# The first FFN product of a hybrid decoder layer, ordered by one event loop

## The chip, the core and the metric

The kernel runs on one core of a Trainium2 chip. The time is device time in microseconds (us) of that core, from launch to end; a median of several runs is compared. Five engines work side by side, each through its own queue in order: TensorE (PE) multiplies matrices, with PEld as its weight load; VectorE (DVE), ScalarE (ACT) and GpSimd (POOL) work elementwise; SyncE (SP) issues most of the memory transfers (DMAs), ACT some of them. SBUF is the on-chip memory of the operands; PSUM holds the products in banks.

## What is computed

One layer on 2048 tokens of width 1024: a norm and a combined projection, three mixers side by side (sliding-window attention, a state-space scan, sparse attention), an output projection, and a feed-forward network (FFN). The part that matters here is the FFN, in float32:

```python
h2 = rms_norm(x, norm2_g[l])
hid = jax.nn.relu(jnp.einsum('bld,df->blf', h2, w_up[l]))        # 2048 x 1024 by 1024 x 4096
x = x + jnp.einsum('blf,fd->bld', hid * hid, w_down[l])          # 2048 x 4096 by 4096 x 1024
```

## The kernel before, in words

**Seven products for eight.** Both FFN products cut their operands in two by two blocks and form seven block products, called "1" to "7" and made in the order `ORDER = "1675243"`. For each, one token operand (a "factor") and one weight operand are needed. Factors "1", "2", "3" are blocks of the normed rows, turned (in memory: `hT`); "4" to "7" are sums of blocks (in memory: `sums`). Weight operands "1", "2", "4" are blocks of `w_up`; the other four are sums that GpSimd forms.

**Three matmuls for one.** A float32 operand is split into a high half in the matmul's rounded format (a cast on ACT) and a low half (source minus high, on DVE). Each 128 by 512 piece of a product is high times high, high times low and low times high. A block product has four such pieces, so twelve matmuls.

**Steps.** The first product (`phase_up`, line 1999) works on 1024 tokens at a time (p = 0, then 1) and 256 columns of `w_up` at a time (f): 32 steps of seven products. For p = 0, f runs downwards, for p = 1 upwards, so that steps 15 and 16 share their weights. The seven factors of a token half stay in SBUF (`fh`, `fl`); the weights of each step are loaded (`ur`, line 2117), summed (`fs`, line 2121) and split (`uh`, `ul`, lines 2128 and 2131). Products go to four banks a, d, c, b in two sets that alternate by step; "1" and "2" share bank a, "7" and "4" bank c, "5" and "3" bank b. The evictions take one bank after another: ACT copies "1" (line 2186), DVE adds the others (`add`, line 2175) into result buffers, ACT or DVE applies relu and square (lines 2178, 2179, 2201, 2202), and GpSimd combines the four results into the factors "5", "6", "7", "3" of the second product (`ev`, line 2182), which go to memory (`vd`, line 2172). The four blocks of results take eight result buffers a step out of ten; three more hold running sums (`eu`).

**The first factors.** A factor is loaded whole, 1 MB, into one of two buffers (`fx`, line 2078). Those of the first three products are split in four pieces of 512 (lines 2086 and 2090, from lines 2084 to 2090 `high` and `low`); the other four of p = 0 are split whole, 2048 wide, by `refill`. At the change of half, `refill` splits the factors of p = 1 as each product of step 15 has released its factor; three of them come in four pieces of 256 KB (`fy`, line 2106) in free weight buffers.

**Rows of the second half.** During the first twelve steps, `fetch` (line 2042) loads normed rows (`fxr`), ACT scales them (line 2050), TensorE turns them (line 2059), ACT scales them again (`fxb`, line 2061), GpSimd forms their sums (`fxt`, line 2071), and SP stores both.

**What sets the order.** The attention and the output projection before the FFN (`phase_mix`, line 1156) are written as tasks of an event loop (`Flow`, line 1067): each task yields operations with an engine and an expected time, and the loop issues whichever operation can start first by these times, the lowest rank first among equals. What it issues stays in that order on each engine (`manual_schedule`). In the kernel before, the loop also takes in the FFN's first pieces: `attention_over` (line 1863), `ffn_factor` (1888), `ffn_weights` (1903), `ffn_kept` (1912) and `ffn_product` (1918), up to step 0's products "1", "6" and "7". The rest of `phase_up` is written as plain loops, and the framework's scheduler chooses the order on each engine. `phase_down` (line 2272), the second product, is left to the scheduler too; its first loads and splits are raised in priority by 1000 instructions (`DOWN_HOIST`), so that they may go between the last instructions of the first product. Its buffers lie on bytes of the first product's.

## Time and profile before

| | us |
|---|---|
| median of 3 runs (2465.37 to 2467.47) | 2465.64 |
| the profiled execution's own time | 2468.63 |
| its span, first to last instruction | 2466.8 |
| TensorE busy in it | 2399.6 |
| first product, 32 steps: from 1196 to 1845 | 649 |
| second product: from 1845 to the end | 622 |

A row of the profile names the engine, the line of the code, the operation and the tiles (written <- read), and how long it took; in square brackets stands how long its engine had been idle before and what it had waited for. `<-DVE fl L2090` means that the last thing to arrive was a tile `fl` written by VectorE at line 2090. Rows of a stretch give each engine's busy time with the number of its instructions that lie in or reach into it, the clock that TensorE was granted (1.00 is full), and the share of DMA time.

### The profile page before, as it was taken

How to read it: one execution, taken by the hardware profiler on the slowest of the kernel's cores; microseconds unless marked ns; L12 is line 12 of the kernel's file. 1: busy time of each engine (PE TensorE's matmuls, PEld its weight loads, DVE VectorE, ACT ScalarE, POOL GpSimd, SP SyncE). 2: the span in 40 equal slices, each digit the busy share in tenths (PEclk: the TensorE clock that was granted, in tenths of full speed). 3: DMA queues.
4: the chain of work that ended last, by engine and by line, in shares of the span. 5: the costliest groups of instructions: out<-in, count | busy, mean ns of one | idle time of the engine just before them, and what ended most of it. 6: DMA issues, size and time to landing. Idle time of an engine off the chain costs nothing.

```text
span 2466.8 us, 37987 instructions
## 1 busy us (share of the span) xinstructions
PE 2399.6 (97%) x12738; PEld 2061.1 (84%) x12738; DVE 1776.0 (72%) x3473; ACT 1322.2 (54%) x2765; POOL 1038.4 (42%) x1070
## 2 busy tenths in 40 slices
PE   8999998999999999999999999999999999999999
PEld 8899998777788888989787788788887888888887
DVE  7853875864687888888656566655558888889886
ACT  6443545765677767666465556444444444434442
POOL 0000223322343454321656674666554544445447
PEclk9999999999899999999999999999999999999999
DMA  7483334441332243211676667655548443444435
GB/s 238 135 259 116 107 93 109 107 152 50 96 97 70 87 129 114 63 44 53 206 221 190 189 197 219 195 154 153 156 129 284 128 124 107 126 135 130 127 102 197
DMA packets 402260, 344.45 MB, mean 140 GB/s; under 512 B 43622, under 2 KB 359020, under 8 KB 400112
## 3 DMA queue, kind: packets, MB, share of 16 engines
q1 hardware_dynamic: 341696, 288.23, 38.8%
q10 hardware_dynamic: 60368, 53.80, 7.0%
q8 instruction: 100, 1.64, 0.3%
q14 instruction: 96, 0.79, 0.1%
HBM read 227.39 MB, written 119.76 MB: 141 GB/s over the span
## 4 chain that ended last, share of the span: by engine, by line
PE 71%; DVE 2%; issue 2%; DMA 2%; POOL 1%; ACT 1%; SPq 0%; ACTq 0%; DVEq 0%; POOLq 0%
PE pdc L2360 7%; PE pdb L2360 7%; PE pda L2360 7%; PE pw L1802 7%; PE pub L2151 6%; PE puc L2151 6%; PE pua L2151 6%; PE pdd L2360 3%; PE pud L2151 3%; PE pos L1497 3%; PE pps L1464 2%; PE pqs L1439 1%; PE pqs L1440 1%; PE pow L1497 1%; PE ppw L1464 1%
## 5 line engine op out<-in xcount | busy, mean ns | idle before, releaser
L1995 ACT CAST v<-vr 128x512 fp32r<-128x512 f32 x224 | 139.2, 623 | 303.9 <-DMA vr<-vd 149.8
L1996 DVE TENSOR_TENSOR v<-vr,v 128x512 fp32r<-128x512 f32 x224 | 240.4, 1082 | 75.3 <-ACT v L1995 75.1
L2360 PE MATMUL pdc<-dw,v 128*128 128x512 f32 x768 | 187.5, 393 | 4.1 <-ACT dw L1995 3.2
L2360 PE MATMUL pdb<-dw,v 128*128 128x512 f32 x768 | 184.5, 389 | 0.0
L2360 PE MATMUL pda<-dw,v 128*128 128x512 f32 x768 | 184.5, 389 | 0.0
L2360 PEld LDWEIGHTS pdc<-dw,v 128*128 128x128 f32 x768 | 145.5, 190 | 35.8 <-ACT dw L1995 3.7
L548 POOL TENSOR_TENSOR t<-Q,E 128x508 f32<-128x508 f32 x16 | 21.3, 1334 | 365.6 <-ACT Q L528 334.7
L2360 PEld LDWEIGHTS pdb<-dw,v 128*128 128x128 f32 x768 | 144.3, 188 | 30.0
L2360 PEld LDWEIGHTS pda<-dw,v 128*128 128x128 f32 x768 | 144.1, 188 | 29.9
L2121 POOL TENSOR_TENSOR fs<-ur,ur 128x512 f32<-128x512 f32 x62 | 92.9, 1499 | 161.1 <-DMA ur<-in_w_up 135.2
L2128 ACT CAST uh<-fs 128x512 fp32r<-128x512 f32 x124 | 76.3, 621 | 152.7 <-PE pub L2151 57.3
L2131 DVE TENSOR_TENSOR ul<-fs,uh 128x512 fp32r<-128x512 f32 x124 | 128.3, 1035 | 38.5 <-ACT uh L2128 38.1
L2131 DVE TENSOR_TENSOR ul<-ur,uh 128x512 fp32r<-128x512 f32 x93 | 96.6, 1040 | 40.4 <-ACT uh L2128 38.6
L1480 ACT CAST ths<-pps 128x512 fp32r<-128x512 f32 (+1 forms) x144 | 78.7, 562 | 67.2 <-PE pps L1464 62.2
L2182 POOL TENSOR_TENSOR ev<-e,e 128x512 f32<-128x512 f32 x64 | 94.5, 1476 | 42.8 <-ACT e L2179 18.5
L1485 DVE TENSOR_TENSOR tls<-pps,ths 128x512 fp32r<-128x512 f32 (+1 forms) x144 | 93.1, 657 | 23.1 <-ACT ths L1480 22.1
L1802 PE MATMUL pw<-wo_h,mh 128*128 128x512 f32 x256 | 106.5, 416 | 1.0 <-DVE mx L1824 0.5
L2151 PE MATMUL pub<-fh,uh 128*128 128x512 f32 x256 | 102.1, 399 | 4.6 <-DVE e L2175 3.0
L1802 PE MATMUL pw<-wo_l,mh 128*128 128x512 f32 x256 | 104.4, 408 | 0.0
L1802 PE MATMUL pw<-wo_h,ml 128*128 128x512 f32 x256 | 103.7, 405 | 0.0
L2151 PE MATMUL pub<-fl,uh 128*128 128x512 f32 x256 | 101.1, 395 | 0.3 <-DVE fl L2090 0.3
L2151 PE MATMUL pub<-fh,ul 128*128 128x512 f32 x256 | 101.0, 394 | 0.0
(583 smaller groups left out, 7778.4 us busy)
## 6 DMA issues: line engine op xcount, KB each, us to landing
vr<-vd SPq DMA_DIRECT2D x224, 256.0 KB
vd<-ev SPq DMA_DIRECT2D x128, 256.0 KB
ur<-in_w_up SPq DMA_DIRECT2D x124, 256.0 KB
vd<-e ACTq DMA_DIRECT2D x64, 256.0 KB
dr<-in_w_down SPq DMA_DIRECT2D x32, 512.0 KB
x<-in_x SPq DMA_DIRECT2D x16, 512.0 KB
mx<-in_x ACTq DMA_DIRECT2D x32, 256.0 KB
x<-mx ACTq DMA_DIRECT2D x32, 256.0 KB
```

The costliest lines, as they stand in the source:

```text
L1480: yield "ACT", cast_ns(n), lambda: nc.scalar.copy(th[:, 0:nb], pt[:, 0:nb])
L1485: t = yield "DVE", sub_ns(n), lambda: nc.vector.tensor_tensor(tl[:, 0:nb], pt[:, 0:nb], th[:, 0:nb], op=ALU.subtract)
L1497: nc.tensor.matmul(po_of(), v_of(b0 + j), tt[:, j].rearrange("p h q -> p (h q)"), start=b0 + j == 0 and n == 0, stop=b0 + j == nblk - 1 an ...
L1802: t = yield "PE", mm_ns(512), lambda: nc.tensor.matmul(pw[n], a[half][:, j], b[k][:, sl], start=k == 0 and m == 0, stop=k == NK - 1 and m ...
L1995: nc.scalar.copy(dh, src)
L1996: nc.vector.tensor_tensor(dl, src, dh, op=ALU.subtract)
L2121: nc.gpsimd.tensor_tensor(S[n], x, y, op=op)
L2128: nc.scalar.copy(res[o][0], source(o))
L2131: nc.vector.tensor_tensor(res[o][1], source(o), res[o][0], op=ALU.subtract)
L2151: nc.tensor.matmul(bank, w[:, k], h[o][:, k], start=first and k == 0 and n == 0, stop=k == HALF - 1 and n == 2, skip_group_check=True)
L2182: nc.gpsimd.tensor_tensor(tile_("v" + o), x, y, op=op)
L2360: nc.tensor.matmul(bank[b, q], x[:, q, j], y[:, j], start=first and j == 0 and n == 0, stop=j == 1 and n == 2, skip_group_check=True)
```

## The change

The generator `phase_up` becomes a class `Up` whose parts are all tasks of the same event loop; the whole first product is now issued in the loop's order.

- **Order of products.** Steps 0 and 1, and steps 16 and 17, are interleaved: three products of the first step, then by turns one of the second and one of the first, then the last three of the second.
- **Factors.** Every factor of both halves is split in four pieces of 512; a product may begin when its first piece is there. In p = 0, all seven are fetched by a task of their own (`first_factors`), each as soon as one of the two buffers is free. In p = 1 (`second_factors`), the fetches begin from step 13 on, when the rows are stored: "1" and "6" whole into the two buffers, "7" and "5" in pieces in weight and sum buffers, "2", "4" and "3" whole as the buffers come free.
- **Weights.** `all_weights` loads those of step n + 1 when step n begins, into the same six buffers; each of the fourteen split halves has a buffer of its own name.
- **Results.** One pool of 13 buffers; seven are used in a step (the running sum is kept in the buffer of result "12", and "7" overwrites it).
- **Rows of the second half.** `sums` loads after the last product of step 3m; scaling and turning are tied to products that are done and to the expected landing. For m = 0 the turning moves to steps 2 and 3.
- **Room.** The output projection's buffers (`late_pool`) are released inside the loop (`late_over`) once every block's rows are stored; the later factors, the result buffers and the second set of banks are laid out then (`rest`). Until then only products "1" and "6" of step 0 may be issued; all evictions wait for it in the loop.

```diff
@@ -1864,62 +1868,26 @@
 
             yield E[NT - 1]["oc"]
             yield R["pt"]
...
             t = yield "SP", 30, switch
             put(R["pt"], t)
             put(R["pw"], t)
...
+            up.begin(flow, E[NT - 1]["mh", 0], t)
+            for i in range(NT):
+                yield E[i]["x1"]
+                if i < NT // 2:
+                    yield E[i]["hT"]
+            yield sums_out
+            t = yield "SP", 30, late_over
+            up.rest(t)
+
+        def late_over():
+            c_late.close()
...
+class Up:
...
+        self.steps = [(0, f) for f in reversed(range(nf))] + [(1, f) for f in range(nf)]
+        self.turned_at = nf
+        self.order = []
+        for n in range(2 * nf):
+            if n in (0, nf):
+                self.order += [(n, 0), (n, 1), (n, 2)] + [x for k in range(4) for x in ((n + 1, k), (n, k + 3))] + [(n + 1, k) for k in (4, 5, 6)]
+            elif n not in (1, nf + 1):
+                self.order += [(n, k) for k in range(7)]
+        self.due = {x: 10 * j for j, x in enumerate(self.order)}
...
+    def begin(self, flow, hold, t):
+        self.flow, self.hold = flow, hold
+        self.hp, self.hh, self.hl = {}, {}, {}
...
+        self.factors(ORDER[:1])
+        self.s = Slots(flow, self.pool("f_st", 5), "s", 5)
+        self.x = Slots(flow, self.pool("f_x", 2), "x", 2)
+        self.ur = Slots(flow, self.pool("f_ru", 6), "ur", 6)
...
+        sp(self.all_weights(), R_FFN, t)
+        sp(self.first_factors(), R_FFN, t)
+        sp(self.products(), 2 * R_FFN, t)
+        sp(self.second_factors(), self.rank(self.turned_at - 1, 0), t)
+        for m in range(4):
+            sp(self.sums(m), self.rank(max(3 * m + 1, 2), 0) + 50, t)
+
+    def rest(self, t):
+        flow = self.flow
+        self.v = Slots(flow, self.pool("f_e", 13), "e", 13)
+        self.g2t = self.pool("f_g", 1).tile([P, PAD], F32, name="f_g2")
+        self.factors(ORDER[3:])
+        self.ps.append(self.pool("f_psu2", 1, space=PSUM))
+        self.nc.sync.dma_start(self.g2t[:, 0:NK], self.g2[0].rearrange("(k p) -> p k", p=P))
+        flow.fire(self.more, t)
...
+    def all_weights(self):
+        flow, made = self.flow, Event()
+        for n in range(len(self.steps)):
+            if n == self.turned_at:
+                continue
+            if n > 1:
+                yield self.began[n - (2 if n in (2, self.turned_at + 1, self.turned_at + 2) else 1)]
+            if n == self.turned_at + 1:
+                yield self.pieces
+            f0 = self.steps[n][1] * FC_UP
+            A = {}
+            for q, uses in (("11", 3), ("21", 2), ("22", 2), ("12", 2)):
+                k, c = int(q[1]) - 1, f0 + P * (int(q[0]) - 1)
+                A[q] = yield from self.ur.get([P, HALF, P], f"ur{n}{q}", uses)
+                t = yield "SP", 60, lambda: self.nc.sync.dma_start(
+                    A[q].tile, self.w_up[0, 512 * k:512 * k + 512, c:c + P].rearrange("(k p) f -> p k f", p=P))
+                A[q].land = self.landing(t, 2.6e5)
+            if n == self.turned_at - 1:
+                flow.fire(self.last_loads, t)
+            flow.spawn(self.weight_sums(n, A), self.rank(n, 1) - 5, t)
+            for o, q in (("1", "11"), ("2", "12"), ("4", "22")):
+                flow.spawn(self.keep(n, o, A[q], A[q].land), self.rank(n, ORDER.index(o)), 0.0)
+
...
+    def weight_sums(self, n, A):
+        S = {}
+        for e in A.values():
+            yield e.land
+        if n == 0:
...
+                                     (3, "11", "21", ALU.subtract, 1, "7"), (4, "12", 2, ALU.subtract, 1, "3")):
+            S[j] = yield from self.s.get([P, HALF, P], f"fs{n}{j}", uses)
+            a, b = S.get(x) or A[x], S.get(y) or A[y]
+            t = yield "POOL", 1400, lambda: self.nc.gpsimd.tensor_tensor(S[j].tile, a.tile, b.tile, op=op)
+            a.drop(t)
+            b.drop(t)
+            e = Event()
+            self.flow.fire(e, t)
+            self.flow.spawn(self.keep(n, o, S[j], e), self.rank(n, ORDER.index(o)), t)
+
...
+    def keep(self, n, o, src, there):
+        yield there
+        yield self.room[o]
+        h, l = self.W[n][o] = [self.up_.tile([P, HALF, P], F32R, tag=q + o, name=f"{q}{n}{o}", bufs=1) for q in ("uh", "ul")]
+        yield "ACT", 621, lambda: self.nc.scalar.copy(h, src.tile)
+        t = yield "DVE", 900, lambda: self.nc.vector.tensor_tensor(l, src.tile, h, op=ALU.subtract)
+        src.drop(t)
+        self.flow.fire(self.made[n][o], t)
+
...
+    def halves(self, p, o, rank, parts):
+        if p:
+            yield self.done[self.turned_at - 1][ORDER.index(o)]
+        elif o in ORDER[3:]:
+            yield self.more
+        h, l = self.hh[p, o], self.hl[p, o] = [self.hp[o].tile([P, HALF, 4, P], F32R, tag=n + o, name=f"f{n}{p}{o}") for n in "hl"]
+        for k in range(HALF):
+            src, x, land = parts[k]
+            yield land
+            t = yield "ACT", 621, lambda: self.nc.scalar.copy(h[:, k], x)
+            self.flow.spawn(self.low_half(p, o, k, src, x, h, l), rank, t)
+
+    def low_half(self, p, o, k, src, x, h, l):
+        t = yield "DVE", 950, lambda: self.nc.vector.tensor_tensor(l[:, k], x, h[:, k], op=ALU.subtract)
+        src.drop(t)
+        self.flow.fire(self.fact[p, o][k], t)
+
+    def whole(self, p, o, rank):
+        src = yield from self.x.get([P, HALF, 4, P], f"fx{p}{o}", HALF)
+        t = yield "SP", 60, lambda: self.nc.sync.dma_start(src.tile, self.source(p, o))
+        land = self.landing(t, 1e6)
+        self.flow.spawn(self.halves(p, o, rank, [(src, src.tile[:, k], land) for k in range(HALF)]), rank, t)
+
+    def in_pieces(self, p, o, slots, rank):
+        parts = []
+        for k in range(HALF):
+            src = yield from slots.get([P, 4, P], f"fy{p}{o}{k}", 1)
+            t = yield "SP", 60, lambda: self.nc.sync.dma_start(src.tile, self.source(p, o)[:, k])
+            parts.append((src, src.tile, self.landing(t, 2.6e5)))
+        self.flow.spawn(self.halves(p, o, rank, parts), rank, t)
...
+    def first_factors(self):
+        for k, o in enumerate(ORDER):
+            yield from self.whole(0, o, self.rank(0, k))
+
+    def second_factors(self):
+        n = self.turned_at - 1
+        yield self.began[n - 2]
+        for e in self.turned:
+            yield e
+        rank = [self.rank(n + 1, k) for k in range(7)]
+        yield from self.whole(1, ORDER[0], rank[0])
+        yield from self.whole(1, ORDER[1], rank[1])
+        yield self.last_loads
+        yield from self.in_pieces(1, ORDER[2], self.ur, rank[2])
+        yield from self.in_pieces(1, ORDER[3], self.s, rank[3])
+        self.flow.fire(self.pieces, 0.0)
+        for k in range(4, 7):
+            yield from self.whole(1, ORDER[k], rank[k])
...
+    def products(self):
+        nc, flow = self.nc, self.flow
+        all_banks = {}
+        for n, k in self.order:
+                p, o = self.steps[n][0], ORDER[k]
+                banks = all_banks.setdefault(n, {})
+                if n or k > 1:
+                    yield self.more
+                yield self.made[n][o]
+                b = "adcbacb"[k]
+                if k < 4:
+                    yield self.bank[b, n % 2]
+                    banks[b] = self.ps[n % 2].tile([P, 4 * P], F32, tag=b, name=f"pu{b}{n}")
+                else:
+                    yield self.seen[n][{"2": "1", "4": "7", "3": "5"}[o]]
+                uh, ul = self.W[n][o]
+                for j in range(HALF):
+                    yield self.fact[p, o][j]
+                    hh, hl = self.hh[p, o], self.hl[p, o]
+
+                    def part():
+                        for i, (w, h) in enumerate(((uh, hh), (uh, hl), (ul, hh))):
+                            nc.tensor.matmul(banks[b], w[:, j], h[:, j], start=k < 4 and j == 0 and i == 0, stop=j == HALF - 1 and i == 2, skip_group_check=True)
+                    t = yield "PE", 3 * mm_ns(512), part
+                    if k == 0 and j == 0:
+                        flow.fire(self.began[n], t)
+                flow.fire(self.done[n][k], t)
+                if n != self.turned_at - 1:
+                    flow.put(self.room[o], t)
+                flow.spawn(self.evicted(n, o, banks[b], b), self.rank(n, k) + 11, t)
...
+    def evicted(self, n, o, pu, b):
+        nc, flow = self.nc, self.flow
+        E, seen = self.e.setdefault(n, {}), self.seen[n]
+        yield self.more
...
+        if o == "1":
+            E["12"] = yield from self.v.get([P, 4 * P], f"ex{n}", 1)
+            t = yield "ACT", 580, lambda: nc.scalar.copy(E["12"].tile, pu)
...
+        elif o in "74":
+            yield seen["6"]
+            name = "22" if o == "7" else "21"
+            E[name] = yield from self.v.get([P, 4 * P], f"e{name}{n}", 2)
+            r = E[name].tile
+            t = yield "DVE", 700, add(r, E["12"].tile)
...
+        for q, x, y, op in (("5", "12", "22", ALU.add), ("6", "v5", "11", ALU.subtract), ("7", "11", "12", ALU.subtract),
+                            ("3", "21", "v6", ALU.subtract)):
+            for g in (x, y):
+                if g in self.value[n]:
+                    yield self.value[n][g]
+            if q == "7":
+                E["v7"] = E["12"]
+            else:
+                E["v" + q] = yield from self.v.get([P, 4 * P], f"ev{q}{n}", 1 if q == "3" else 2)
+            t = yield "POOL", 1400, lambda: nc.gpsimd.tensor_tensor(E["v" + q].tile, E[x].tile, E[y].tile, op=op)
+            for g in (x, y):
+                if g != "12":
+                    E[g].drop(t)
+            flow.spawn(self.posted(n, q, E["v" + q]), self.rank(n, 6) + 11, t)
+
+    def posted(self, n, q, slot):
...
+    def sums(self, m):
+        nc, flow = self.nc, self.flow
+        yield self.done[3 * m][6]
+        raw = yield from self.x.get([P, 2, NK, P], f"fxr{m}", 1)
...
+                nc.sync.dma_start(raw.tile[:, b].rearrange("p k t -> p (k t)"), self.x1[i * P:i * P + P])
+        t = yield "SP", 120, load
+        yield self.landing(t, 1e6)
+        for b in range(2):
+            yield self.done[3 * m + 1][1 + 2 * b] if m else self.done[2][b]
+            r = raw.tile[:, b].rearrange("p k t -> p (k t)")
+            yield "ACT", 1110, lambda: nc.scalar.activation(r, r, AF.Copy, scale=self.rr[:, 8 + 4 * b + m:9 + 4 * b + m])
+        B = {}
+        for j, (b, k) in enumerate(((0, 0), (1, 0), (1, 1), (0, 1))):
+            n, at = (((3 * m + 1, 5), (3 * m + 2, 0), (3 * m + 2, 2), (3 * m + 2, 4)) if m else ((2, 2), (2, 4), (3, 2), (3, 4)))[j]
+            yield self.done[n][at]
+            if j == 0:
+                box = yield from self.x.get([P, 4, HALF, P], f"fxb{m}", 1)
+            bank = self.bank["d", 1 - n % 2]
+            yield bank
...
-        up = phase_up(tc, C, x1, rr, norm2_g, hT, sums, w_up, vd)
-        phase_mix(tc, C, x, gains, B, cmp, w_out, gs[:, 1], gs[:, 0], pd, oa_d, ob, x1, hT, sums, rr, rh_c, ss_a, ss_b, r_d, oc_d, rest, c_u.close, c_b.close, up)
-        for _ in up:
-            pass
+        with ExitStack() as c_f:
+            up = Up(tc, c_f, C, x1, rr, norm2_g, hT, sums, w_up, vd)
+            phase_mix(tc, C, x, gains, B, cmp, w_out, gs[:, 1], gs[:, 0], pd, oa_d, ob, x1, hT, sums, rr, rh_c, ss_a, ss_b, r_d, oc_d, rest, c_u.close, c_b.close, up)
```

Of the FFN, the arithmetic and the number of matmuls, splits, sums and stores by element are the same; `phase_down` is not edited.

More of the change, by code (lines that the diff above doesn't have):

```diff
@@ L1944, in block_sums @@
                 put(R["xt"], s + DMA_NS)
+            left_sums.pop()
+            if not left_sums:
+                fire(sums_out, s)
         with tc.manual_schedule():
@@ L1980 @@
 R_FFN = 100000
+FC_UP = 256
 R_GLU = 150
```

410 lines of the change are left out of this document (139 added, 271 removed).

## The prediction

> **What bounds the kernel now.** I read the page first, then the busy time by stretches, then TensorE's timeline, and last the other engines' timelines where TensorE stood.
>
> ```profile
> span 2466.8 us, 37987 instructions
> PE 2399.6 (97%) x12738; PEld 2061.1 (84%) x12738; DVE 1776.0 (72%) x3473; ACT 1322.2 (54%) x2765; POOL 1038.4 (42%) x1070
> core 0: us, PE busy (x) PEld busy (x) DVE busy (x) ACT busy (x) POOL busy (x), PEclk, DMA share, GB/s
> 1209.60:1248.55 38.95, 35.12 (x131) 25.65 (x130) 31.89 (x30) 23.40 (x35) 22.56 (x20) 0.87 0.71 228
> 1340.15:1355.63 15.48, 13.70 (x61) 11.01 (x60) 4.74 (x7) 5.88 (x10) 8.49 (x7) 1.00 0.94 268
> 1401.07:1416.90 15.83, 13.89 (x61) 11.18 (x61) 5.31 (x7) 6.07 (x10) 8.11 (x7) 1.00 0.88 256
> 1546.00:1562.47 16.47, 13.48 (x52) 10.61 (x52) 8.87 (x9) 5.92 (x10) 13.99 (x10) 0.90 0.77 229
> 1565.19:1835.00 269.81, 269.81 (x1193) 223.39 (x1192) 157.65 (x185) 129.65 (x213) 163.75 (x112) 1.00 0.51 149
> 1845.19:1868.80 23.61, 19.52 (x73) 14.85 (x72) 20.95 (x19) 13.22 (x20) 13.34 (x7) 0.86 0.84 272
> ```
>
> In the chain of work that ended last:
>
> ```profile
> 1567.91 2.72 PE pub L2151 x12
> ```
>
> TensorE is the bound: 97% busy, and the change takes no matmul away. So all that can be won is time in which TensorE doesn't run at its pace. The chain's row gives the pace: twelve matmuls in 2.72 us, 0.2267 each. In the 269.81 us of the second token half nothing is lost at all. What a stretch loses is its length less 0.2267 for each matmul begun in it. The count includes one that only reaches in, so I take one off:
>
> - opening of the first product: 38.95 - 130 x 0.2267 = 9.5 us
> - two places where the second half's rows are turned: 15.48 - 60 x 0.2267 = 1.9, and 15.83 - 60 x 0.2267 = 2.2, together 4.1
> - the change of token half: 16.47 - 51 x 0.2267 = 4.9
> - the start of the second product, whose code isn't edited: 23.61 - 72 x 0.2267 = 7.3
>
> The first three make 18.5 us: that is the most the edited stretches can give, 0.75% of the span.
>
> ```profile
> 1218.25 0.51 PE L2151 MATMUL puce<-fl,uh 128*128 128x512 f32 x1 [1.93 <-DVE fl L2090]
> 1222.53 0.80 PE L2151 MATMUL pub<-fh,uh 128*128 128x512 f32 x1 [1.60 <-ACT fh L2086]
> 1223.13 0.63 PE L2151 MATMUL pua<-fh,uh 128*128 128x512 f32 x1
> ...
> 1227.59 0.63 PE L2151 MATMUL pub<-fl,uh 128*128 128x512 f32 x1
> 1228.02 0.63 PE L2151 MATMUL pub<-fh,ul 128*128 128x512 f32 x1
> ...
> 1352.60 0.50 PE L2151 MATMUL puc<-fh,uh 128*128 128x512 f32 x1 [1.78 <-DVE eu L2175]
> ...
> 1555.09 0.50 PE L2151 MATMUL pub<-fh,uh 128*128 128x512 f32 x1 [2.99 <-DVE e L2175]
> ```
>
> The waits are short, but after those at 1218 to 1223 the matmuls start 0.43 us apart (1227.59, 1228.02) instead of 0.23, and the page of stretches has a granted clock of 0.87 and 0.90 around the opening and the change of half, 1.00 around the two middle ones. So a wait of 3 us there costs 4.9, and one of 1.8 (1352.60) costs only itself. The Trainium skill, "TensorE: Matmul & The Clock Gate", Part 1, has the clock halve after an idle window of about 3.4 us; here 2.99 us was enough, so the measurement decides, and by the page's figure the turn of halves would be worth some 1.9 us less.
>
> **What made TensorE wait.** The rows of the engines in front of it:
>
> ```profile
> 1207.24 7.90 SPq L2117 DMA_DIRECT2D ur<-in_w_up  x3
> ...
> 1217.68 0.63 ACT L1827 ACTIVATE junk<-mx 128x512 f32<-128x512 f32 x1 [5.85 <-DVE mx L1824]
> ...
> 1347.83 1.15 ACT L2050 ACTIVATE fxr<-fxr,rr 128x1024 f32<-128x1024 f32 x1 [6.98 <-DMA fxr<-x]
> 1551.01 0.62 ACT L2128 CAST uh<-fs 128x512 fp32r<-128x512 f32 x1 [7.71 <-POOL fs L2121]
> ...
> 1542.44 1.72 POOL L2182 TENSOR_TENSOR ev<-e,e 128x512 f32<-128x512 f32 x1 [16.21 <-DMA vd<-e]
> ```
>
> Opening: the load of factor "5" is SP's next instruction after three weight loads that hold it 7.90 us, waiting for buffers, and ScalarE stands 5.85 us for the last block's addition. Middle: ScalarE stands 6.98 us for rows from memory, with weight casts and evictions queued behind it. Change of half: GpSimd forms the next weights only after result sums that kept it idle 16.21 us; ScalarE stands 7.71 us for them, VectorE behind it holds an eviction, TensorE waits for that bank. All three are orders in queues, not lack of engine time over the whole phase (VectorE 157.65 of 269.81 in the steady stretch).
>
> **The change, part by part.**
>
> *Interleaving of two steps.* In the opening this is less than it says: the rows at 1222.53 (pub, step 0) and 1223.13 (pua, step 1) show that the present order already mixes them. What is new there is the exact order, one factor for every two products, and factors "5", "2", "4", "3" cut in 16 pieces of 512 instead of four of 2048. Pieces let a product begin after a quarter of a split, but they cost VectorE:
>
> ```profile
> L2090 DVE TENSOR_TENSOR fl<-fx,fh 128x2048 fp32r<-128x2048 f32 x4 | 9.2, 2293 | 5.3 <-ACT fh L2086 5.3
> L2090 DVE TENSOR_TENSOR fl<-fx,fh 128x512 fp32r<-128x512 f32 x4 | 4.9, 1219 | 1.3 <-ACT fh L2086 1.3
> ...
> 1180.00:1209.60 29.60, 3.19 (x4) 1.00 0.53 178
> 1209.60:1248.55 38.95, 13.31 (x13) 0.87 0.71 228
> ...
> L2131 DVE TENSOR_TENSOR ul<-fs,uh x124: 676/946/1804, 1201.4 to 1827.0; 128x512 fp32r<-128x512 f32 x124
> L2175 DVE TENSOR_TENSOR e<-pub,eu x64: 677/692/692, 1230.4 to 1845.4; 128x512 f32<-128x512 f32 x64
> ...
> L2090 DVE TENSOR_TENSOR fl<-fx,fh 128x2048 fp32r<-128x2048 f32 x4 | 10.5, 2623 | 3.8 <-ACT fh L2086 3.8
> L2090 DVE TENSOR_TENSOR fl<-fy,fh 128x512 fp32r<-128x512 f32 x12 | 7.5, 680 | 0.0
> ```
>
> The first two and the last two rows are the factor splits of the opening and of the change of half; the windowed pair is the weights' low halves (L2131). A subtraction of 512 from two SBUF operands takes from 0.68 to 1.80 us; the additions that read a bank never pass 0.69. The Trainium skill, "SBUF — State Buffer", section "SBUF: two separate sides", says that VectorE instructions with two SBUF inputs and GpSimd instructions hold a shared port in turn, each for a whole instruction. By that rule 16 entries are worse than four; the spread of the rows agrees, and it makes the first rival below.
>
> Call a piece's price x. Opening: VectorE did 31.89 us; of the 4 + 13 low halves 14 belong to steps 0 and 1, so three, 3.1 us, are for step 2 and can go later. Without the 9.2 for the large splits, 31.89 - 3.1 - 9.2 + 16x = 19.6 + 16x, against 130 x 0.2267 = 29.5 us of matmuls. TensorE loses at least 16x - 9.9. x lies between 0.68 (loss 1.0) and 1.80 (18.9); I take 13.31 / 13 = 1.02, the nearest kind of operation in the same stretch. Loss 6.4, so the opening gives 9.5 - 6.4 = **3.1**.
>
> *Early fetches.* "5" no longer needs to queue behind the 7.90 us (it can go when the split of "6" frees its buffer). That removes the wait at 1222.53; it can't remove the one at 1218.25, which comes from the last block's addition and its own product's split. I book nothing beyond the 3.1: VectorE is what ends late next.
>
> *Turning the rows.* Scaling is placed after the rows' expected landing instead of after a place in the program. Bounds: nothing to 4.1, or 1.9 to 2.2 below nothing, by one more such wait. I take **3.5**, as ScalarE has 52% of its time free (129.65 of 269.81 busy) and a scaling that comes later holds nobody.
>
> *Change of half.*
>
> ```profile
> 1516.58:1555.09 38.51, 35.52 (x157) 29.09 (x155) 27.98 (x31) 23.07 (x33) 18.45 (x12) 1.00 0.72 224
> ```
>
> In this stretch, with the columns of the first table, VectorE works 27.98. Cutting four large splits: 27.98 - 10.5 + 16x = 17.5 + 16x, against 35.5 us of matmuls (38.51 less the 3.0 idle). At 1.02 it is 33.8, at the 0.68 that the pieces took in this very stretch 28.4: it fits below x = 1.12. Interleaving moves step 17's first weights behind three products of step 16, and gives each later factor two products. So the 4.9 should go; I keep 0.5 for orders that the planner misjudges: **4.4**.
>
> *Seven result buffers a step.* Thirteen buffers, as ten and three before, and in-place additions of the same length, and the same stores. No time; they'd cost if a store landed late, and then the result sums on GpSimd wait, which now have 106 us free of 269.81.
>
> *What else moves.* Each weight load, store and sum now has a fixed place on SP and GpSimd. A late one holds those behind it. In the steady stretch VectorE, ScalarE and GpSimd have 39% or more to spare, which covers that; without that cover each 0.5 us a step would cost 14 us over 28 steps. The second product's opening stays at 7.3, by 7.3 either way at most: its hoisted loads and splits are still the scheduler's to place between the fixed instructions.
>
> Sum: 3.1 + 3.5 + 4.4 = 11.0 us. The profiled execution took 2468.63 (span 2466.8 and 1.8 around it), 3.0 above the median of 2465.64. So 2468.6 - 11.0 = 2457.6 for such an execution, and 2465.6 - 11.0 = **2454.6** for the median, rounded to 2455.
>
> **Rivals.**
>
> *VectorE paces both interleaved stretches* (slower). If pieces and GpSimd's sums take turns throughout, x nears 1.80: the opening loses 18.9, the change of half 17.5 + 28.8 - 35.5 = 10.8, together 29.7 against 18.5 now, +11.2: 2477. It decides from x where 16x - 9.9 + 16x - 18.0 = 18.5, at 1.45 us. For: the four pieces of the opening took 1.22 on average and GpSimd was busy 22.56 of 38.95. Against: 0.68 in the change of half, while GpSimd stood still.
>
> *The orders change, the waits stay* (the change doesn't do what it says). The opening is already mixed, and its first wait hangs on the old block's addition; the change of half gets a new order with a wait like the old. Then only the middle's 4.1 goes: 2461.5.
>
> *Everything goes.* x at 0.68 and the second product's start better covered: up to 18.5 + 7.3 = 25.8, 2440. Against: nothing in the diff aims at that start.
>
> **How the numbers follow.** Forecast 0.53; waits stay 0.19; everything goes, 2440 to 2448, 0.13; slower 0.15. This kernel's measurement tells about 0.2%, 4.9 us, from no change. The forecast and the larger gain count as faster, with 0.01 of the stays: 0.67. The rest of the stays is within 0.2%: 0.18. Slower 0.15. The range runs from 2443, most of the larger gain, to 2470, the stays with a small loss beside them; it leaves out the slow rival's far end and the lowest times.
>
> **What would show it.** Right: a stretch of the opening that loses 5 to 8 us with VectorE above 90% and factor pieces near 1.0 us; no wait over 1 us in the two middle places; a change of half with a clock of 1.00. Wrong: pieces above 1.45 us; waits of TensorE in the steady stretch of the second half, which has none now; a start of the second product that loses more than 10 us, its splits no longer placed ahead of the last products.

## The result and the profile after

The changed kernel takes 2449.51 us (median of 4 runs, 2448.93 to 2452.78) against 2466.19 (4 runs, 2465.37 to 2467.47): a ratio of 0.9935, with a 95% interval of 0.9917 to 0.9952. The medians differ by 16.7 us, and the ratio says 0.65% less; 11.0 us less was forecast.

The page of the kernel after, its two lines that answer to those of before:

```profile
span 2447.7 us, 37971 instructions
PE 2392.3 (98%) x12738; PEld 2056.7 (84%) x12738; DVE 1765.2 (72%) x3497; ACT 1319.8 (54%) x2789; POOL 1026.8 (42%) x1070
```

The same 12738 matmuls, with 7.3 us less of PE time and a span that is 19.1 shorter in these two executions. Four stretches of the kernel after (opening; 50 us around the change of half; the steady second half; start of the second product):

```profile
core 0: us, PE busy (x) PEld busy (x) DVE busy (x) ACT busy (x) POOL busy (x), PEclk, DMA share, GB/s
1206.96:1245.71 38.75, 37.16 (x158) 28.91 (x156) 36.17 (x47) 24.99 (x46) 22.44 (x20) 1.00 0.60 186
...
1525.00:1575.00 50.00, 49.96 (x219) 40.54 (x217) 37.27 (x43) 21.26 (x38) 32.47 (x22) 1.00 0.63 189
1575.11:1825.30 250.19, 250.19 (x1104) 207.30 (x1105) 136.19 (x172) 118.52 (x199) 147.41 (x104) 1.00 0.52 153
1825.50:1849.20 23.70, 19.63 (x73) 14.90 (x72) 20.88 (x19) 13.11 (x20) 12.40 (x7) 0.86 0.84 279
```

By the prediction's rule (length less 0.2267 for each matmul begun) the opening loses 38.75 - 157 x 0.2267 = 3.2 instead of 9.5, the 50 us around the change of half 50.00 - 218 x 0.2267 = 0.6 instead of 4.9, and the start of the second product 23.70 - 72 x 0.2267 = 7.4, as before. The clock is 1.00 in every stretch of the first product. TensorE's own waits in the kernel after, from its timeline:

```profile
1216.65 0.50 PE L2209 MATMUL pub<-fl,uh 128*128 128x512 f32 x1 [0.33 <-DVE fl L2149]
...
1229.03 0.51 PE L2209 MATMUL puc<-fl,uh 128*128 128x512 f32 x1 [0.85 <-DVE fl L2149]
...
1834.02 1.22 PE L2429 MATMUL pdc<-dw,v 128*128 128x512 f32 x2 [2.94 <-ACT dw L1967]
1836.11 4.58 PE L2429 MATMUL pdc<-dw,v 128*128 128x512 f32 x10 [0.87 <-DVE dw L1968]
```

The first two are the opening's longest that are left, and both name VectorE's factor split. The last two are the untouched start of the second product.

**Where the time went.** For all kernels below I use one measure beside the total. The *first product's length* runs from the start of the output projection's last matmul to the start of the second product's first. Within it, a *loss* is the sum of the intervals between the starts of neighbouring matmuls beyond 0.2267 us (0.0885 for a transpose). The opening is the first 45 us of the length, the middle the next 255, the change of half the next 100; the start of the second product is its first 40 us. The middle holds 2.0 in each of the nine kernels with no wait in it, so only what goes beyond that counts. What is left of the length loses nothing, but for one kernel named below.

| | length | opening | middle | change of half | start of second product |
|---|---|---|---|---|---|
| before (1209.37 to 1845.19) | 635.82 | 9.8 | 6.6 | 4.9 | 7.4 |
| after (1206.74 to 1825.48) | 618.74 | 3.4 | 2.0 | 0.9 | 7.5 |

The length falls by 17.1: 6.4 in the opening, 4.6 in the middle, 4.0 at the change of half, together 15.0. The other 2.0 are nine matmuls of the first product that now run earlier, between those of the output projection. In the kernel before three matmuls fit there (1196.32 to 1196.87), and then TensorE waited:

```profile
1198.11 0.66 PE L1765 MATMUL ptx<-c_ident,mix 128*128 128x128 f32 x4 [0.85 <-DVE ml L1768]
```

In the kernel after twelve run there, the first and the last of them:

```profile
1192.08 0.39 PE L2209 MATMUL pua<-fh,uh 128*128 128x512 f32 x1
...
1195.06 0.40 PE L2209 MATMUL pua<-fh,ul 128*128 128x512 f32 x1
```

The two executions' spans differ by another 2.0: the work ahead of the first product ended 2.6 us earlier, and what follows it took 0.6 more. The code ahead is hardly edited, and its end lies between 1203.1 and 1210.8 over the profiled executions of the kernel after and its variants, between 1206.0 and 1209.4 for the kernel before and its two. So a single time carries some us that belong to no edit, and the experiments are read by the length and the losses.

### The profile page after: what moved, and what is told of

It reads as the page before. It is cut to its first block, busy times and chain, and to the rows that moved or that the text cites. A ratio compares the mean times of both kernels' runs of the same rounds, so it can differ in the third digit from the quotient of the medians.

```text
span 2447.7 us, 37971 instructions
## 1 busy us (share of the span) xinstructions
PE 2392.3 (98%) x12738; PEld 2056.7 (84%) x12738; DVE 1765.2 (72%) x3497; ACT 1319.8 (54%) x2789; POOL 1026.8 (42%) x1070
## 5 line engine op out<-in xcount | busy, mean ns | idle before, releaser
L2131 DVE TENSOR_TENSOR ul<-fs,uh 128x512 fp32r<-128x512 f32 x124 | 112.3, 924 | 102.9 <-ACT uh L2130 102.8
L2131 DVE TENSOR_TENSOR ul<-ur,uh 128x512 fp32r<-128x512 f32 x93 | 89.9, 969 | 71.0 <-ACT uh L2130 69.5
L2278 POOL TENSOR_TENSOR ev<-ex,e 128x512 f32<-128x512 f32 x32 | 43.1, 1347 | 206.4 <-ACT ex L2261 195.0
L2261 ACT ACTIVATE e<-e 128x512 f32<-128x512 f32 x128 | 81.0, 633 | 58.0 <-DVE e L2230 55.9
L2209 PE MATMUL puc<-fl,uh 128*128 128x512 f32 x256 | 100.0, 391 | 1.1 <-DVE fl L2149 0.9
```

The source lines that it names most:

```text
L2131: t = yield "DVE", 900, lambda: self.nc.vector.tensor_tensor(l, src.tile, h, op=ALU.subtract)
L2209: nc.tensor.matmul(banks[b], w[:, j], h[:, j], start=k < 4 and j == 0 and i == 0, stop=j == HALF - 1 and i == 2, skip_group_check=True)
L2261: t = yield "ACT", 640, lambda: nc.scalar.activation(r, r, func)
L2278: t = yield "POOL", 1400, lambda: nc.gpsimd.tensor_tensor(E["v" + q].tile, E[x].tile, E[y].tile, op=op)
```

## The experiments

My theory A: VectorE's time for the factor splits paces the opening, and the orders in the queues set the rest. Each experiment names its rival B. A single time stands for each of these ten, with the kernel before at 2465.2 to 2468.0 beside them; two more kernels, with several times each, come at the end. All but the two named so are edits of the kernel after. The kernel without the low halves computes something else, and serves for its timeline alone.

| kernel | us | length | opening | middle | change of half | start of second product |
|---|---|---|---|---|---|---|
| no interleaving | 2467.27 | 636.48 | 13.3 | 2.0 | 8.6 | 7.3 |
| splits of 2048 | 2451.0 | 621.71 | 6.2 | 2.0 | 1.1 | 7.3 |
| 16 low halves twice | 2459.76 | 631.24 | 12.6 | 5.5 | 0.6 | 7.5 |
| 16 low halves left out | 2446.68 | 616.17 | 0.8 | 2.0 | 0.9 | 7.5 |
| before, in pieces | 2467.18 | 636.70 | 10.7 | 5.3 | 6.2 | 7.5 |
| before, sums first | 2464.62 | 635.12 | 9.6 | 6.3 | 4.7 | 7.5 |
| late fetch | 2450.54 | 620.18 | 3.4 | 2.0 | 2.3 | 7.5 |
| no wait for landing | 2454.96 | 621.59 | 3.4 | 3.7 | 1.9 | 7.5 |
| sums behind | 2453.61 | 622.48 | 3.4 | 2.0 | 4.6 | 7.5 |
| weight splits first | 2453.49 | 618.81 | 3.4 | 2.0 | 0.9 | 7.5 |

### No interleaving

```
-            if n in (0, nf):
+            if False:
                 self.order += [(n, 0), (n, 1), (n, 2)] + ...
-            elif n not in (1, nf + 1):
+            else:
                 self.order += [(n, k) for k in range(7)]
```

> The changed kernel with its products in plain order: step 1 after step 0, step 17 after step 16; pieces, fetches and all else as changed. A, VectorE paces the opening: the same subtractions have to be done, but step 0 now asks for all sixteen pieces of factors 5, 2, 4, 3 within four products (10.9 us of matmuls for sixteen pieces of 0.8 us and the evictions), so the opening loses 7 to 10 us where the changed kernel loses 3.1, with some matmuls at half clock; the change of half, with 2.72 us a product against four pieces of 0.8 to 1.2, loses 3 to 8 where it loses nothing now. B, interleaving adds little, since the kernel before already mixed the first two steps: both stretches within 1 us of the changed kernel's.

The length is 636.48, back at the kernel before's 635.82, although the event loop, the seven buffers, the early fetches and the pieces are all there. The opening loses 13.3 and the change of half 8.6; both are more than in the kernel before (9.8 and 4.9) and beyond A's ranges. Its TensorE waits over 1 us at both places:

```profile
1216.60 0.58 PE L2209 MATMUL pub<-fh,uh 128*128 128x512 f32 x1 [2.87 <-ACT fh L2145]
...
1226.26 0.50 PE L2209 MATMUL puc<-fh,uh 128*128 128x512 f32 x1 [2.00 <-ACT fh L2145]
1230.43 0.79 PE L2209 MATMUL puc<-fl,uh 128*128 128x512 f32 x1 [3.67 <-DVE fl L2149]
...
1549.42 0.50 PE L2209 MATMUL pub<-fh,uh 128*128 128x512 f32 x1 [1.65 <-ACT fh L2145]
1552.80 0.80 PE L2209 MATMUL pub<-fl,uh 128*128 128x512 f32 x1 [2.88 <-DVE fl L2149]
```

All five name a factor (fh, fl): with one product to each factor, the splits end later than TensorE needs them. So without the interleaving nothing of the gain is left at either place: 10.0 and 7.8 us against the kernel after. At the change of half the kernel before has the plain order too. In the opening it doesn't: it mixes two steps there already, so the 10.0 us are what mixing is worth, not what the change added to it. The middle keeps its gain without it.

### Splits of 2048, and twice or never the low halves

Three edits of the split of factors "5", "2", "4", "3" in the first half, where the kernel after makes 16 pieces. Whole splits as in the kernel before:

```
+        if not p and o in ORDER[3:]:
+            src, _, land = parts[0]
+            yield land
+            t = yield "ACT", 1900, lambda: self.nc.scalar.copy(h, src.tile)
+            t = yield "DVE", 2600, lambda: self.nc.vector.tensor_tensor(l, src.tile, h, op=ALU.subtract)
```

> The changed kernel with factors 5, 2, 4, 3 of the first token half split whole (one cast and one subtraction of 2048) instead of in four pieces each. A, VectorE's time paces the opening: four subtractions of 2.3 us, 9.2 in all, stand for sixteen of 0.82, 13.1, so VectorE has 3.9 us less to do; only the latency of a whole split (1.9 and 2.3 us before a product may begin) speaks against it; the opening loses 1 to 5 us, about as much as with pieces (3.1). B, pieces are what brought the gain, since a product can begin after a quarter: the opening loses 7 us or more.

The same 16 low halves computed twice:

```
-        t = yield "DVE", 950, lambda: ...tensor_tensor(l[:, k], x, h[:, k], op=ALU.subtract)
+        for again in range(2 if not p and o in ORDER[3:] else 1):
+            t = yield "DVE", 950, lambda: ...tensor_tensor(l[:, k], x, h[:, k], op=ALU.subtract)
```

> The changed kernel with each of the sixteen low halves of factors 5, 2, 4, 3 of the first token half computed twice, into the same place. A, VectorE paces the opening: sixteen more subtractions of 0.82 us are 13.1 us, of which the 2.6 us that VectorE has free in that stretch (36.17 busy of 38.75) take some; the opening loses 3.1 + 13.1 - 2.6 = 13.6 us, 10 to 16. B, the opening's loss is the latency of two late factors: VectorE's surplus goes into later steps and the opening loses 3 to 6.

The same 16 left out; the matmuls that should read them read the high halves:

```
+        if not p and o in ORDER[3:]:
+            h = self.hh[p, o] = self.hl[p, o] = self.hp[o].tile(...)
...
+            if not p and o in ORDER[3:]:
+                src.drop(t)
+                self.flow.fire(self.fact[p, o][k], t)
+                continue
```

> The changed kernel without the low halves of factors 5, 2, 4, 3 of the first token half: the matmuls that would read them read the high halves again, so TensorE's work is the same and VectorE is spared sixteen subtractions, 13 us. A, VectorE paces the opening: the opening's loss of 3.1 us falls below 1.2; what is left is the start of product 7, which waits for the last block's addition. B, the loss comes from late loads or from ScalarE's order: it stays at 2.5 to 3.5.

The last two agree with A. Without the 16 low halves the opening loses 0.8; with 16 more it loses 9.2 us more. (The doubled kernel's middle loses 3.5 more as well, in three waits for additions. The first ends at 1351.22, over 100 us after the last doubled piece, so these are no part of the pieces' price; I take them for other orders that the loop chose, which isn't shown.) The opening's stretches of these two, the doubled first:

```profile
1205.50:1250.00 44.50, 37.58 (x142) 24.96 (x141) 42.04 (x57) 23.07 (x43) 17.13 (x17) 1.00 0.45 145
```

```profile
1207.30:1246.00 38.70, 38.50 (x169) 31.19 (x167) 26.05 (x32) 24.36 (x46) 18.31 (x20) 1.00 0.57 187
```

VectorE (the third busy column) is 94% busy in the first, and TensorE waits for it; in the second it is 67% busy and TensorE never stops. That shows the opening to be paced by VectorE.

The whole splits disagree with the simple form of A. The four (minimum, median and maximum in ns):

```profile
L2146 DVE TENSOR_TENSOR fl<-fx,fh x4: 2280/2293/3370, 1216.6 to 1232.9; 128x2048 fp32r<-128x2048 f32 x4
```

They take VectorE some 10.2 us (3 x 2.29 + 3.37), less than 16 pieces at 0.79 (the kernel after's, below), and yet the opening lost 2.8 more: 6.2, between A's 1 to 5 and B's 7. Its waits, and the split that the second one names:

```profile
1216.67 0.50 PE L2218 MATMUL pub<-fh,uh 128*128 128x512 f32 x1 [1.42 <-ACT fh L2145]
1218.99 0.69 PE L2218 MATMUL pub<-fl,uh 128*128 128x512 f32 x1 [1.82 <-DVE fl L2146]
```

```profile
1216.65 2.29 DVE L2146 TENSOR_TENSOR fl<-fx,fh 128x2048 fp32r<-128x2048 f32 x1 [1.11 <-ACT fh L2145]
```

The first matmul may start when ScalarE has cast the whole factor, the next when VectorE has finished all 2.29 us of it (1216.65 to 1218.94). A piece releases the first matmul after a quarter of that. So it is the pace of VectorE together with the delay of a large split. All other parts of the change, with whole splits, have 3.6 of the opening's 6.4 already; the pieces add the other 2.8.

### Before, in pieces

```
-            for k in range(HALF) if isinstance(rows[o], list) else (None,):
+            for k in range(HALF):
```

> The kernel before with one part alone: all factors that it splits whole are split in four pieces of 512; order and fetches stay the framework's. A, the opening is a matter of VectorE's time and of the order: pieces alone bring VectorE up to 4 us more work; the opening loses 8 to 12 us, against 9.5 before, and the change of half 3 to 6, against 4.9. B, pieces bring the gain of the opening: it loses 3 to 5 us.

In the kernel before, pieces alone bring nothing (opening 10.7 for 9.8, change of half 6.2 for 4.9). Here A is right: pieces alone don't bring the gain; they need the rest of the change beside them.

### GpSimd's order at the change of half

The prediction read this wait as one of order on GpSimd: result sums first, the next weights' sums behind them. First, the kernel before with the loads and sums for step 17 written ahead of step 16's products:

```
+            if n == NF:
+                load, order, keep_high, keep_low, first_u = weight_steps(*steps[n + 1])
+                load()
+                for _, sums_of in order:
+                    if sums_of is not None:
+                        sums_of()
```

> The kernel before with one part alone: the weights of step 17 are loaded and summed ahead of step 16's products in the program, so that GpSimd need not do them after the result sums. A, the change of half was an order in GpSimd's queue: its loss of 4.9 us falls below 1, all else within 1 us of before. B, the weights were late because their loads or buffers were: the loss stays at 3 to 5.

The loss stayed, but so did the order. GpSimd's timeline in that kernel:

```profile
1538.59 1.72 POOL L2182 TENSOR_TENSOR ev<-e,e 128x512 f32<-128x512 f32 x1 [16.21 <-DMA vd<-e]
...
1543.20 1.29 POOL L2182 TENSOR_TENSOR ev<-e,ev 128x512 f32<-128x512 f32 x1
1544.45 1.28 POOL L2121 TENSOR_TENSOR fs<-ur,ur 128x512 f32<-128x512 f32 x1
```

The scheduler still put the weights' sums (fs) behind the result sums (ev), so this run tells nothing about the order. In the kernel after the order is the other way round, three of the four fs first:

```profile
1520.98 1.61 POOL L2119 TENSOR_TENSOR fs<-ur,ur 128x512 f32<-128x512 f32 x1 [11.70 <-DMA vd<-e]
...
1525.97 1.73 POOL L2278 TENSOR_TENSOR ev<-ex,e 128x512 f32<-128x512 f32 x1
```

So I gave the kernel after the old order:

```
         if n == 0:
             yield self.hold
+        if n == self.turned_at + 1:
+            yield self.summed
...
+        if n == self.turned_at - 1:
+            flow.fire(self.summed, t)
```

> Kernel after, with the weight sums of step 17 held on GpSimd until the result sums of step 15 are done, which is the order that the kernel before had at the change of half. Theory A (the interleaving, one factor for every two products, is what took the loss away; the order of GpSimd is not what decides): the change of half loses 0.5 to 2 us as in the kernel after (0.8), and the first product takes 618 to 621 us. Rival B (GpSimd's order was the cause, as the prediction's reading of the 7.71 us and 16.21 us rows had it): ScalarE waits for GpSimd again there, the change of half loses 3.5 to 5.5 us, and the first product takes 622 us or more.

The change of half loses 4.6 instead of 0.9: the rival is right and A, which thought the interleaving enough, wrong. GpSimd's rows in that kernel:

```profile
1523.21 1.55 POOL L2280 TENSOR_TENSOR ev<-ex,e 128x512 f32<-128x512 f32 x1 [12.96 <-ACT ex L2263]
...
1529.83 1.74 POOL L2121 TENSOR_TENSOR fs<-ur,ur 128x512 f32<-128x512 f32 x1
```

And TensorE's rows:

```profile
1537.85 0.50 PE L2211 MATMUL pud<-fh,ul 128*128 128x512 f32 x1 [2.72 <-DVE ul L2133]
1538.19 0.40 PE L2211 MATMUL pud<-fh,uh 128*128 128x512 f32 x1
...
1539.13 0.53 PE L2211 MATMUL pud<-fl,uh 128*128 128x512 f32 x1
1539.45 0.63 PE L2211 MATMUL pud<-fh,ul 128*128 128x512 f32 x1
...
1542.44 0.49 PE L2211 MATMUL pua<-fh,uh 128*128 128x512 f32 x1
```

The first fs comes at 1529.83 instead of 1520.98, its low half (ul) is late, TensorE waits 2.72, and the half clock follows. The run without interleaving had the good order and lost 8.6 all the same, to the factors:

```profile
1531.99 1.34 POOL L2119 TENSOR_TENSOR fs<-ur,ur 128x512 f32<-128x512 f32 x1 [11.93 <-DMA vd<-e]
...
1536.70 1.73 POOL L2278 TENSOR_TENSOR ev<-ex,e 128x512 f32<-128x512 f32 x1
```

So the change of half needs both: the weights' sums ahead of the old step's result sums, and the time of two products for each new factor. Neither alone is enough.

### Late fetch, and no wait for landing

```
     def second_factors(self):
-        yield self.began[n - 2]
+        yield self.done[n][0]
```

> The changed kernel with the factors of the second token half fetched only when step 15's first product is done, not from step 13 on. A, early fetches matter because a factor has to be there when its predecessor is released: the first factors then land 5 to 7 us after the release (1 MB each, two at a time), all splits shift by that much, and with VectorE busy in most of this stretch the change of half loses 2 to 8 us where it loses nothing. B, interleaving gives enough room (the first split has 16 us of other products in front of it): it loses under 1 us.

The change of half loses 2.3 for 0.9. As a loss that is within A's 2 to 8; but A took it to be nothing in the kernel after, and the early fetch is worth 1.4 us, less than A meant and more than B.

```
         t = yield "SP", 120, load
-        yield self.landing(t, 1e6)
```

> The changed kernel with the scaling of the second half's rows issued by place alone, not after the rows' expected landing. A, the middle waits were ScalarE standing at a load that had not landed, with evictions behind it: one to three of the four places get back a wait of 1.5 to 2.5 us, 2 to 6 us in all. B, the loads go out early enough now that the landing no longer matters: under 1 us in all.

The number is A's: 1.7 more in the middle and 1.1 more at the change, together 2.8. The reason isn't. What ScalarE stood idle for at the rows' scaling, in the kernel before (busy line, then idle time and count by releaser):

```profile
L2050 ACT ACTIVATE fxr<-fxr,rr x8: 1137/1152/1154, 1240.7 to 1410.8; 128x1024 f32<-128x1024 f32 x8
...
  DMA fxr<-x: 21.2, 5
```

In the kernel after:

```profile
L2303 ACT ACTIVATE fxr<-fxr,rr x8: 1146/1150/1158, 1249.1 to 1415.8; 128x1024 f32<-128x1024 f32 x8
...
  POOL fs L2119: 5.0, 1
```

The 21.2 us behind the rows' loads, at five of the eight scalings, are gone, and with them TensorE's waits of 1.78 and 1.94. But in the kernel without the wait for landing they stay gone:

```profile
L2302 ACT ACTIVATE fxr<-fxr,rr x8: 1148/1150/1155, 1252.6 to 1422.3; 128x1024 f32<-128x1024 f32 x8
...
  POOL fs L2119: 5.2, 1
```

There the scalings still come behind the same weight casts, since each also waits for a product further on. What the edit changed is the loop's reckoning of when ScalarE is free, and so the order of other casts and activations; the new waits name an addition and a weight's cast:

```profile
1405.43 0.50 PE L2209 MATMUL pub<-fh,uh 128*128 128x512 f32 x1 [0.60 <-DVE e L2230]
...
1561.56 0.50 PE L2209 MATMUL pub<-fh,uh 128*128 128x512 f32 x1 [0.81 <-ACT uh L2130]
```

So the scaling's place behind that product suffices to keep the waits for the rows away. The place did it, and not an earlier load: the third pair of rows is loaded at 1343.1 and 1343.8 in the kernel before and scaled at 1347.8 and 1349.5; in the kernel after it is loaded at 1343.5 and 1344.0 and scaled at 1350.7 and 1357.0. That the expected landing is what keeps the other orders good is argued, not shown.

### The start of the second product

This part isn't edited, and is now the largest loss left (7.5). The third weight's cast comes late there. I tried three ways to bring it forward. The weight splits of the first three products written ahead of the token splits:

```
+            for o in ORDER[:3]:
+                first[o]()
             for k in range(AHEAD):
                 tokens(k)
-                first[ORDER[k]]()
-            for o in ORDER[AHEAD:]:
-                first[o]()
+                if k > 1:
+                    first[ORDER[k + 1]]()
+            first[ORDER[6]]()
```

> Kernel after, with the weight splits of the second product's first three products moved ahead of the token splits in its opening. Theory A (the 7.0 us that the start of the second product loses come from one weight cast, the third, that stands on ScalarE behind token casts; its data and its buffer are there some 15 us before): the wait of 2.94 us and the half clock behind it go, the start loses 2 to 4.5 us, and the kernel takes 2446 to 2449 us. Rival B (the splits ahead of the first products are as many as before, so a token split is late in place of the weight): the start loses 6 to 9 us, and the time stays within 2 us of the kernel after's.

The start loses 7.5, as in the kernel after: B's number, but the cast stands in the same place among ScalarE's instructions as in the kernel after, so the edit did not reach what it was made for. Then two orders of the buffers in memory, which do move the cast:

```
         v_high = pool("d_v2", 5)
+        w_high = pool("d_w2", 5)
         ep = pool("d_e", 4)
-        w_high = pool("d_w2", 5)
```

> Kernel after, with the second product's five later weight buffers laid out ahead of its four eviction buffers in memory, so that they come free with another tile of the first product; the rest is unchanged. Theory A (the 7.0 us that the start of the second product loses hang on where the third weight's buffer lies, because that sets when its cast and low half are placed on ScalarE and VectorE): the cast is now ahead of the last result's activation, the wait of 2.94 us goes, the start loses 2 to 5 us, and the kernel takes 2444.5 to 2447.5 us. Rival B (VectorE does all splits of the start in a row and is its bound, whatever stands first: a token split or a later sum is late in place of the weight): the start loses 6 to 9 us, and the time is within 2 us of the kernel after's 2449.5.

```
+        w_high = pool("d_w2", 5)
         v_high = pool("d_v2", 5)
         ep = pool("d_e", 4)
-        w_high = pool("d_w2", 5)
```

> Kernel after, with the same five weight buffers laid out ahead of the five token buffers and the four eviction buffers, which lets token splits be placed earlier still and puts the five weight splits in one row behind them. Theory A: the start of the second product loses 2 to 6 us, and the kernel takes 2444.5 to 2448.5 us. Rival B (VectorE is the bound of the start; and a token split that is placed ahead of the first product's last additions holds these while its rows are still on their way from memory): the start loses 7 us or more and the end of the first product begins to lose too, 2449 to 2454 us.

They took 2455.0 us (5 runs, ratio to the kernel before 0.9954, 0.9937 to 0.9972) and 2460.32 us (9 runs, 0.9970, 0.9958 to 0.9982). Both are slower than the kernel after, against A and by more than B: the first is beyond its 2 us, the second beyond its 2454. In the first the old wait is gone and others stand in its place:

```profile
1835.10 4.60 PE L2429 MATMUL pda<-dw,v 128*128 128x512 f32 x12 [2.19 <-ACT acc0u L2435]
1843.02 2.93 PE L2429 MATMUL pdd<-dw,v 128*128 128x512 f32 x6 [3.32 <-ACT v L1967]
```

The first loses 12.5 at that start, the second 13.8, and another 1.5 in the last 5 us of the first product, as B said of it. The weights' casts now stand ahead of the last result's activation on ScalarE: in the first kernel it comes 8.1 us after the second product's first matmul, in the kernel after 1.5 us. ScalarE then waits 2.35 us for token rows (vr) that came late from memory; that the late activation held them is argued. The other kernels lose 7.3 to 7.5 there, whichever wait is the longest. That ScalarE and VectorE are the bound there, whatever the order, is not shown; other orders weren't tried. The kernel after stays the fastest complete one of this study.

## Why the prediction was right, and where it was not

*The bound.* Right: TensorE's losses in the named places went, and nothing came back elsewhere. The steady second half still has none (250.19 busy of 250.19), and the second product's start, taken at nothing, stayed: 7.4 before, 7.5 after.

*The opening* was forecast to give 3.1 and gave 6.4. The step that failed is "I take 13.31 / 13 = 1.02" for the price of a piece: the factor pieces cost less than the weights' low halves of the old trace. The opening of the kernel after, VectorE's factor splits alone:

```profile
core 0: us, DVE busy (x), PEclk, DMA share, GB/s
1206.96:1245.71 38.75, 15.60 (x19) 1.00 0.60 186
```

15.60 / 19 = 0.82, with the last pieces of "7" among the 19. The sixteen that the formula prices took 0.79 on average: fourteen 0.67 to 0.70, one 1.34, one 1.77. 16 x 0.79 - 9.9 = 2.7, near the 3.2 that the stretch lost. That it comes so near is in part luck, since VectorE did more there than the formula counted (36.17 us, 93%, and 47 instructions); the mechanism stands on the doubled and the omitted low halves. The Trainium skill, "SBUF — State Buffer", section "SBUF: two separate sides", has such subtractions wait for whole GpSimd instructions. The trace agrees: the two pieces of "7" that ran beside GpSimd's sums took 1.77 and 1.78. But with GpSimd busy 22.44 of 38.75 us only two of the sixteen paid for it, and the average stayed far from the rival's 1.80.

*What interleaving does in the opening:* "In the opening this is less than it says" holds. From 1222.53 on, the old trace too has matmuls of one product of step 1 beside each of "5", "2", "4" and "3", and after 1229.05 it loses only 0.9; 8.9 of its 9.8 are lost before that, at "7" and at "5". The new order differs there in that step 1's first product runs whole ahead of "5", which gives the split of "5" some 2.7 us more (twelve matmuls). Taking all mixing away costs 10.0, so the mixing has to stay; but it was not new.

*Early fetches* were booked at nothing beyond that, and the wait at 1218.25 was said to be out of their reach. It went all the same: its loss of 2.1 is 0.3 now. At the change of half they are worth 1.4, within the 4.4 booked there. In the opening the trace shows what is earlier now. VectorE's low halves of "7" begin at 1201.87, 5.1 us before the opening's first matmul; in the kernel before they began at 1210.21, 0.6 us behind it, taking turns with GpSimd's sums (1.71 and 1.77 us for the first two), and TensorE waited for the third. ScalarE's cast of "5" began at 1220.58 there, 11.0 us behind that matmul, with its data just landed; now it begins 8.2 us behind it, right after the last block's addition, which ScalarE still waits for:

```profile
1214.06 0.63 ACT L1830 ACTIVATE junk<-mx 128x512 f32<-128x512 f32 x1 [5.58 <-DVE mx L1827]
...
1215.16 2.18 ACT L2145 CAST fh<-fx 128x512 fp32r<-128x512 f32 x4
```

SP fetches "7" and "5" ahead of the weight loads; before, the load of "5" went out at 1215.24, behind three of them:

```profile
1191.08 5.32 SPq L2155 DMA_DIRECT2D fx<-sums  x2
1200.04 5.17 SPq L2100 DMA_DIRECT2D ur<-in_w_up  x4
```

How much of the 6.4 is due to the fetches and how much to the order of the products stays open: the fetches were not undone there, and the plain order takes away more than the change brought.

*Turning the rows:* 3.5 forecast of 4.1; the middle gave 4.6. The waits for the rows went, as forecast, though the place behind a later product was enough for that.

*Change of half:* 4.4 forecast, 4.0 measured, for the reasons given there: the order on GpSimd (3.7 when undone) and time for the factors (7.8 when undone). The two are not to be added: each alone brings the loss back.

*Not foreseen:* nine more matmuls between the output projection's, worth 2.0 in the first product's length. Sum: 6.4 + 4.6 + 4.0 + 2.0 = 17.0 against 11.0, and 16.7 in the medians. That the medians come so near the sum is partly luck, as single times carry some us that belong to no edit. *Buffers and fixed places in the queues* cost nothing that the trace shows.

Of the signs to look for, no wait over 1 us in the middle, a clock of 1.00 at the change and VectorE above 90% in the opening were there; the opening's 5 to 8 us and pieces near 1.0 us were not. None of the signs of a wrong prediction appeared.

## What to carry to other kernels

Where an engine that prepares operands falls behind TensorE only for some tens of us, at the start of a phase, look for an order in which a product on an operand that is already there stands between two that each need a new one; and cut the preparation so that the first product can begin after a part of it. Look also at what the preparation itself queues behind: here the load of one factor stood behind three weight loads. A cure may bring nothing by itself, and two late operands (the factors and the weights' sums here) must both be cured before the wait goes. When a piece of work is to be moved, look in the new trace whether it did move: two of the edits here changed the program's text and not the order on the engine.

## What the runs showed of the hardware

TensorE's clock halved after a wait of 2.72 us, and not at once: in the kernel with the sums behind, matmuls start 0.23 us apart until 1539.13, 0.43 apart from 1539.45 to 1542.44, then 0.23 again, so some 3.3 us at half speed that begin 1.3 to 1.6 us after the wait is over. Waits of 1.78 and 1.94 us alone, in the middle of the kernel before, were not followed by it. But one of 1.96 us, at the same place in the kernel with the sums first, was, and at once: the matmuls start 0.43 us apart from 1349.40 to 1352.82, then 0.33 and 0.23.

```profile
1349.40 0.64 PE L2151 MATMUL puc<-fh,uh 128*128 128x512 f32 x1 [1.96 <-DVE eu L2175]
1349.83 0.63 PE L2151 MATMUL puc<-fl,uh 128*128 128x512 f32 x1
```

So the length of a wait near 2 us doesn't settle it, nor when the slow stretch begins. The Trainium skill, "TensorE: Matmul & The Clock Gate", Part 1, has a free-running window of 3.4 us that must pass idle. The length of the slow stretches, some 3.3 and 3.4 us, and their varying beginning agree with such a window; the 2.72 and 1.96 us of idling do not.
